# Gated linear attention: each head's scores from its own 32 partitions, four token tiles at once, in place of block-diagonal queries

## The chip, the cores and the metric

The kernel runs on one core of one Trainium2 chip. The metric is the device time of one execution in microseconds (us). Three runs of the kernel before took 2882.11, 2879.14 and 2889.37 us; their median is 2882.11 us.

## The reference, cut to what matters

The program is a chain of transformer layers over 512 tokens of 1024 features: two hybrid layers ("block 1"), then two further layers with a second stream of 256 context tokens. The change touches one part of each of the two hybrid layers, the gated linear attention of four heads with 32 key features and 64 value features each:

```python
def gated_linear_attention(q, k, v, log_a):      # S = 512, H = 4, Dk = 32, Dv = 64
    qc, kc, vc, gc = to_chunks(q * (Dk ** -0.5)), to_chunks(k), to_chunks(v), to_chunks(log_a)
    def step(state, inp):
        b = jnp.cumsum(gi, axis=2)
        rel = b[:, :, :, None, :] - b[:, :, None, :, :]
        decay = jnp.where(causal, jnp.exp(jnp.minimum(rel, 0.0)), 0.0)
        sc = jnp.einsum('bhid,bhijd,bhjd->bhij', qi, decay, ki)
        intra = jnp.einsum('bhij,bhjv->bhiv', sc, vi)
        inter = jnp.einsum('bhid,bhdv->bhiv', qi * jnp.exp(b), state)
        ...
```

So the score of query i and key j of a head is a sum over 32 features of q times k times a decay that differs by feature and by the pair (i, j), for j not after i; the output is these scores times the values.

## The kernel before, in words

All large products are done in float32r as three matmuls: an operand x is split into a high part (ScalarE casts it, `split`, lines 389 to 394) and a low part (x minus the high part, on GpSimd by line 385 or on VectorE by line 387), and high*high, high*low and low*high are added up in PSUM (`mms`, line 378). Line 376 is the one matmul call of all of them, so groups are told apart by their tiles.

In `layer1` (line 1187) the projections, the retention heads and the gated linear attention of a hybrid layer are laid out together: `weave` (called at line 1258) takes the steps of two generators in turn, `gla` against a chain of `project1`, `project2` and `retention`. The numbers there say how many steps each is reckoned to have, and how far ahead some may be scheduled. With every step `tick` (line 347) also lays out some of the background work, the modulations: `mods` (line 689) brings rows of a weight matrix through three buffers `mr` (one DMA of 256 KB each, line 702) and multiplies them on VectorE (`dot`, line 679). Every engine, and the queue SP that issues all these DMAs, works off its own list in order.

`gla` (line 999) holds queries and keys as [128 = (head, 32 features), 512 tokens]. Decays between two tokens of one tile of 128 tokens are made from seven levels of halving, and an eighth part (level 7 in the code) is the diagonal itself. For a level, keys and queries are multiplied by their decay factors (GpSimd, `prod`, line 1074), and all scores of the level are computed and the right ones kept by a mask: `copy_predicated` (line 1093) takes them from PSUM into A, a tile `oy` of [128 keys, 4 heads x 128 queries] for each token tile.

The heads share the 128 partitions, so the queries are spread out: `level` (line 1050) writes each head's 32 partitions of the queries into its own 128 columns of a tile `qb` that is zero elsewhere (four casts on ScalarE at line 1058, four subtractions on VectorE at line 1059, each 32 partitions x 256). `pair` (line 1062) then multiplies 128x128 keys by 128x512 block-diagonal queries, three matmuls for the four heads of one token tile, into one PSUM bank of the tag "b". `diagonal` does two token tiles at a time (HT = 2), 16 of these half levels in all, each one's matmuls laid out after the next one's preparation (`lagged`, line 302). The four tiles `qb` are filled with zeros first (line 1025). Six further pairs of token tiles (query tile after key tile) are computed the same way, without a mask (lines 1098 to 1115). At last the scores are split in two parts and multiplied by the values (lines 1117 to 1121) into two wide PSUM tiles (tag "s", two banks each, two of them), whose two halves of rows are added by `halves` (lines 883 and 886).

The PSUM tags are shared: "b" (two banks) also takes the scores of `retention` (line 1144) and the decay sums (line 1035); "s" also takes `dense_tok` (line 427), which in `project1` holds both wide tiles at once; "d" takes the projections and the sums of `retention`. In all, `gla` lays out 22 steps per layer.

Of the kernel before, what the change touches and what calls it, by code (L numbers as in the profile page):

```python
# [24 lines left out]
S = 512  # L25
# [9 lines left out]
# column offsets of the projections  # L35
# [70 lines left out]
# 1 / 10000 ** linspace(0, 1, 32) as float32 arithmetic gives it  # L106
# [13 lines left out]
def _consts():  # L120
# [17 lines left out]
    # rows are queries, columns keys  # L138
# [49 lines left out]
class Net:  # L188
# [40 lines left out]
    def area(self, pool, name, **bufs):  # L229
        """Allocator of a stream's attention tiles, by kind."""  # L230
# [5 lines left out]
    def flat(self, shape):  # L236
        """A bank of a wide tile."""
# [64 lines left out]
    def lagged(self, blocks, front=0, back=0):  # L302
        """blocks: generators of two steps; each one's second step comes after the next one's first."""
# [30 lines left out]
    def ahead(self, n):  # L334
        """What is laid out inside may be scheduled n instructions ahead of its place."""
# [11 lines left out]
    def tick(self):  # L347
        """Advances the work in the background."""
# [9 lines left out]
    def stage(self, low=3, **ahead):  # L358
        """low: one of so many low parts of weights is the vector engine's; how far ahead some kinds of work may go."""
# [22 lines left out]
    def lo(self, out, src, hi, scale=1.0, eng="pool"):  # L382
        """out = src * scale - hi"""
# [12 lines left out]
    def split_ps(self, src, hi, lo, scale=1.0):  # L396
        """The source lies in PSUM."""
# [16 lines left out]
    def dense(self, src, h, T, ks=range(KD), tag="d"):  # L414
        """One tile of 128 output features: [128, T] in PSUM."""
# [11 lines left out]
    def dense_tok(self, src, h, T, n, per):  # L427
        """n output features with tokens on partitions: a [128, n] PSUM view per token tile."""
# [16 lines left out]
    def three(self, ps, w, hs):  # L445
        """w: (hi, lo) stationary operands per k tile; hs: (hi, lo) moving ones."""
# [7 lines left out]
    def rstd_cols(self, sq_tiles, T, groups, width, add=False, al=None):  # L454
        """rstd per token (and per group of features) with tokens on partitions: [128, T/128, n]."""
# [17 lines left out]
    def spread(self, cols, T, reps=None, al=None):  # L473
        """[128, T] PSUM tile: per-token values of [128, T/128, n] in every row of their group."""
# [1450 lines left out]
```

## Time and profile before

| | before |
|---|---|
| median of three runs | 2882.11 us (2879.14 to 2889.37) |
| profiled execution, span | 2893.2 us |
| instructions | 33615 |
| TensorE busy (matmul) | 2371.8 us, 82% |
| VectorE busy | 1634.0 us, 56% |
| ScalarE busy | 1171.0 us, 40% |
| GpSimd busy | 1125.4 us, 39% |
| mean granted TensorE clock | 0.896 |

The profile tells one execution, whose only time is its span, 11.1 us (0.4%) above the median of the runs. Its shares are averages over stages with different limits. A matmul's recorded duration includes the pipeline behind it, so the pace of matmuls is read from the distance between their starts, not from their durations. A wait names what ended it last; what ended it may have been held up by something else.

### The profile page before, as it was taken

How to read it: one execution, taken by the hardware profiler on the slowest of the kernel's cores; microseconds unless marked ns; L12 is line 12 of the kernel's file. 1: busy time of each engine (PE TensorE's matmuls, PEld its weight loads, DVE VectorE, ACT ScalarE, POOL GpSimd, SP SyncE). 2: the span in 40 equal slices, each digit the busy share in tenths (PEclk: the TensorE clock that was granted, in tenths of full speed). 3: DMA queues.
4: the chain of work that ended last, by engine and by line, in shares of the span. 5: the costliest groups of instructions: out<-in, count | busy, mean ns of one | idle time of the engine just before them, and what ended most of it. 6: DMA issues, size and time to landing. Idle time of an engine off the chain costs nothing. (4 is left out here: it accounts for less than half of the span.)

```text
span 2893.2 us, 33615 instructions
## 1 busy us (share of the span) xinstructions
PE 2371.8 (82%) x11676; PEld 1960.4 (68%) x11676; DVE 1634.0 (56%) x2822; ACT 1171.0 (40%) x2167; POOL 1125.4 (39%) x754
## 2 busy tenths in 40 slices
PE   5866687668888876668999888999878969799997
PEld 4654565556667665457998776788766757588886
DVE  8777697267747897356452697622635647421212
ACT  3433264334537533345554522222434536332222
POOL 3445245325533652122444742333541221433334
PEclk9978698889979876779999998999988979899999
DMA  6553554354344544324654556632443254332322
GB/s 237 189 182 117 177 169 151 117 161 145 114 118 142 187 160 156 107 92 118 184 156 146 175 172 211 208 95 88 158 136 98 87 159 113 113 113 98 96 95 73
DMA packets 190111, 405.70 MB, mean 140 GB/s; under 512 B 21011, under 2 KB 62453, under 8 KB 186613
## 3 DMA queue, kind: packets, MB, share of 16 engines
q1 hardware_dynamic: 189940, 403.55, 43.4%
q8 instruction: 93, 1.52, 0.2%
q14 instruction: 78, 0.63, 0.1%
HBM read 345.08 MB, written 58.39 MB: 139 GB/s over the span
## 5 line engine op out<-in xcount | busy, mean ns | idle before, releaser
L385 POOL TENSOR_TENSOR wl<-wr,wh 128x1024 fp32r<-128x1024 f32 (+3 forms) x245 | 547.2, 2235 | 839.3 <-ACT wh L409 486.0
L409 ACT CAST wh<-wr 128x1024 fp32r<-128x1024 f32 (+3 forms) x367 | 353.7, 964 | 621.5 <-PE d L376 273.5
L376 PE MATMUL d<-hh,wh 128*128 128x512 f32 x960 | 402.6, 420 | 50.5 <-ACT wh L409 28.9
L376 PE MATMUL d<-hl,wh 128*128 128x512 f32 x960 | 401.0, 418 | 10.5 <-POOL hl L385 7.7
L679 DVE SCALAR_TENSOR_TENSOR mr<-mr,row 128x512 f32<-128x512 f32 x256 | 229.7, 905 | 76.9 <-DMA mr<-in_ada_w 39.0
L376 PEld LDWEIGHTS d<-hh,wh 128*128 128x128 f32 x960 | 194.5, 203 | 98.1 <-ACT wh L409 31.1
L376 PE MATMUL d<-hh,wl 128*128 128x512 f32 x960 | 256.7, 397 | 4.7 <-DVE wl L387 3.4
L387 DVE SCALAR_TENSOR_TENSOR wl<-wr,wh 128x1024 fp32r<-128x1024 f32 (+3 forms) x122 | 154.2, 1264 | 165.5 <-PE d L376 93.1
L376 PEld LDWEIGHTS d<-hl,wh 128*128 128x128 f32 x960 | 193.8, 202 | 56.5 <-POOL hl L385 12.6
L376 PEld LDWEIGHTS d<-hh,wl 128*128 128x128 f32 x960 | 181.9, 191 | 44.3 <-DVE wl L387 5.3
L387 DVE SCALAR_TENSOR_TENSOR pg<-b,pg 128x512 fp32r<-128x512 f32 (+1 forms) x208 | 136.9, 664 | 64.5 <-ACT pg L391 63.0
L892 POOL TENSOR_TENSOR oy<-pg,pg 64x256 f32<-64x256 f32 (+1 forms) x72 | 65.6, 911 | 273.9 <-DVE pg L890 123.5
L376 PE MATMUL b<-hh,wh 128*128 128x512 f32 x416 | 165.4, 398 | 0.0
L376 PE MATMUL b<-hl,wh 128*128 128x512 f32 x416 | 164.4, 395 | 0.0
L391 ACT CAST pg<-b 128x512 fp32r<-128x512 f32 (+1 forms) x208 | 117.3, 570 | 87.5 <-PE b L867 80.4
L840 DVE TENSOR_REDUCE sm<-s 128x1 f32<-128x768 f32 (+3 forms) x144 | 120.5, 845 | 57.0 <-PE s L376 56.5
L679 DVE SCALAR_TENSOR_TENSOR mj<-mr,row 128x512 bf16<-128x512 f32 x128 | 113.0, 882 | 34.5 <-DMA mr<-in_ada_w 34.5
L376 PE MATMUL d<-hc,wh 128*128 128x256 f32 x656 | 106.1, 314 | 26.3 <-ACT wh L409 12.3
L376 PE MATMUL d<-hid,wh 128*128 128x512 f32 (+1 forms) x528 | 116.9, 366 | 10.0 <-ACT hid L391 6.0
L376 PE MATMUL b<-qb,pg 128*128 128x512 f32 x228 | 80.5, 462 | 46.7 <-DVE oy L1093 13.7
L376 PEld LDWEIGHTS d<-hc,wh 128*128 128x128 f32 x656 | 96.0, 216 | 30.8 <-ACT wh L409 13.7
L376 PE MATMUL b<-hh,wl 128*128 128x512 f32 x416 | 108.6, 403 | 9.9 <-DVE wl L387 9.9
(414 smaller groups left out, 5210.5 us busy)
## 6 DMA issues: line engine op xcount, KB each, us to landing
wr<-in_ffn_w_in SPq DMA_DIRECT2D x132, 512.0 KB
mr<-in_ada_w SPq DMA_DIRECT2D x192, 256.0 KB
wr<-in_ffn_w_out SPq DMA_DIRECT2D x48, 512.0 KB
x<-x SPq DMA_DIRECT2D x20, 1024.0 KB
wr<-in_w_in SPq DMA_DIRECT2D x38, 512.0 KB
mr<-in_w_mod SPq DMA_DIRECT2D x64, 256.0 KB
wr<-in_ev_w_in SPq DMA_DIRECT2D x20, 512.0 KB
wr<-in_ffn_w_out SPq DMA_DIRECT2D x24, 384.0 KB
```

The source lines that it names most:

```text
L376: self.nc.tensor.matmul(out, lhsT, rhs, start=start, stop=stop)
L385: self.nc.gpsimd.tensor_sub(out, src, hi)
L387: self.nc.vector.scalar_tensor_tensor(out, src, scale, hi, op0=ALU.mult, op1=ALU.subtract)
L391: self.nc.scalar.copy(hi, src)
L409: nc.scalar.copy(hi[:, :n], raw[:, :n])
L679: self.nc.vector.scalar_tensor_tensor(junk, w, 0.5, v, op0=ALU.mult, op1=ALU.mult, accum_out=out)
L840: nc.vector.reduce_max(c, s, axis=AX.X, negate=True)
L892: nc.gpsimd.tensor_tensor(d, sel(t), sel(rs), op=ALU.mult)
```

## The change

`gla` is written anew from its zero tile on. No block-diagonal queries are made: the level's keys and queries of all four token tiles are split whole (128 x 512, four instructions), and a matmul reads 32 partitions of keys and 32 of queries, one head at a time, into 128 columns. Two heads (`y`: heads 0 and 1, or 2 and 3) and four token tiles fill a wide PSUM tile of the tag "s", and one `copy_predicated` of 128 x 1024 takes it. The six pairs of different token tiles are made two heads at a time in banks of the tag "b", and their parts are gathered by key tile (384, 256 and 128 queries). The scores tile `acc` is now laid out by head. The number of steps stays 22: 16 and 2 times 3. The rest of the diff takes out comments and an unused variable. Its core:

```diff
-        HT = 2
-        qblk = [[self.tl(ph, [128, HT, 4, 128], F32R, f"qb{i}{j}", 1) for i in range(2)] for j in range(2)]
-        for qb in qblk:
-            for q_ in qb:
-                for t in range(HT):
-                    nc.vector.tensor_copy(q_[:, t], A[0])
+        new_r = lambda: self.tl(ph, [128, S], F32R, "gh", 8)
+        new_z = lambda: self.tl(ph, [128, NT, 128], F32, "z", 2)
...
         def level(zk, zq):
-            kh, kl = self.pg([128, N2], F32R), self.pg([128, N2], F32R)
+            kh, kl, qh, ql = (new_r() for _ in range(4))
             self.split(zk, kh, kl)
-            qb = qblk[count[0] % 2]
-            count[0] += 1
-            for h in range(4):
-                r = slice(32 * h, 32 * h + 32)
-                nc.scalar.copy(qb[0][r, :, h, :], v4(zq[r]))
-                self.lo(qb[1][r, :, h, :], v4(zq[r]), qb[0][r, :, h, :], eng="dve" if h in [0, 1, 2, 3] else "pool")
-            return kh, kl, qb
-
-        def pair(lv, jk, jq):
-            kh, kl, qb = lv
-            ps = self.bank([128, 4, 128])
-            c = slice(jk * 128, jk * 128 + 128)
-            fl = lambda a: a.rearrange("p h t -> p (h t)")
-            self.mms(fl(ps), [(kh[:, c], fl(qb[0][:, jq])), (kh[:, c], fl(qb[1][:, jq])), (kl[:, c], fl(qb[0][:, jq]))])
-            return ps
+            self.split(zq, qh, ql, 1.0, "dve")
+            return (kh, qh), (kh, ql), (kl, qh)
+
+        def scores(lv, outs, jk, jq, n, first, last):
+            for i, (a, b) in enumerate(lv):
+                for h, o in outs:
+                    r = slice(32 * h, 32 * h + 32)
+                    self.mm(o, a[r, tok(jk)], b[r, tok(jq, n)], first and i == 0, last and i == 2)
...
-            for t in range(HT):
-                nc.vector.copy_predicated(A[t0 + t], m, pair(lv, t, t))
-
-        yield from self.lagged(diagonal(lvl, t0) for lvl in (7, 0, 1, 2, 3, 4, 5, 6) for t0 in range(0, NT, HT))
+        def diagonal(lvl, lv, y):
+            w = self.wide()
+            for t in range(NT):
+                scores(lv, [(2 * y + x, w[:, x, tok(t)]) for x in range(2)], t, t, 1, t == 0, t == NT - 1)
+            m = self.gla_mask[:, lvl, None, :].to_broadcast([128, 2 * NT, 128])
+            v8 = lambda a: a.rearrange("p h (t i) -> p (h t) i", i=128)
+            nc.vector.copy_predicated(v8(acc[:, 2 * y:2 * y + 2, :]), m, v8(w))
+
+        fs, last = {}, None
+        for lvl in (7, 0, 1, 2, 3, 4, 5, 6, None):
+            lv = None if lvl is None else prepare(lvl)
+            if last is not None:
+                for y in range(2):
+                    diagonal(*last, y)
+                    yield
+            last = lvl, lv
...
+        parts = [((0, 0, 1), (2, 2, 2)), ((3, 2, 2),), ((1, 1, 1),)]
+        for y in range(2):
+            sums = self.wide()
+            hs = (2 * y, 2 * y + 1)
+            v = lambda t, h: gv[t][:, h].rearrange("p a d -> p (a d)")
+            for h in hs:
+                hl = new_r(), new_r()
+                self.split(acc[:, h, :], *hl)
+                for t in range(NT):
                     for i in range(2):
-                        self.mm(acc[h // 2][:, h % 2, q0:q0 + n], v, hl[i][:, h, :],
-                                jt == 0 and i0 == 0 and i == 0, jt == NT - 1 and i == 1)
-                yield
-        for h in range(4):
-            self.halves(acc[h // 2][:, h % 2, :], [(o[h // 2][64 * (h % 2):64 * (h % 2) + 64], lambda a: a)], S)
+                        self.mm(sums[:, h % 2, tok(t)], v(t, h), hl[i][:, tok(t)], t + i == 0, False)
+            yield
+            for jt in range(3):
+                n = (3 - jt) * 128
+                ps = [self.bank([128, n]) for _ in hs]
+                c = 0
+                for jk, jq, m in parts[jt]:
+                    scores(lv, [(h, ps[x][:, c:c + m * 128]) for x, h in enumerate(hs)], jk, jq, m, c == 0, c + m * 128 == n)
+                    c += m * 128
+                for x, h in enumerate(hs):
+                    hl = self.pg([128, n], F32R), self.pg([128, n], F32R)
+                    self.split_ps(ps[x], *hl)
+                    for i in range(2):
+                        self.mm(sums[:, h % 2, (jt + 1) * 128:], v(jt, h), hl[i], False, jt == 2 and i == 1)
+                if jt == 0:
+                    yield
+            for h in hs:
+                self.halves(sums[:, h % 2, :], [(o_[h // 2][64 * (h % 2):64 * (h % 2) + 64], lambda a: a)], S)
+            yield
```

## Rows read from the trace of the kernel before

**Rows 1.** The page's groups: the matmuls with block-diagonal queries, both layers (count, busy us, mean ns).

```profile
L376 PE MATMUL b<-qb,pg 128*128 128x512 f32 x228 | 80.5, 462 | 46.7 <-DVE oy L1093 13.7 <-DVE qb L387 11.8 <-ACT f L1039 11.8
```

**Rows 2.** Busy us by engine in both stages; then clock, DMA share, GB/s.

```profile
105.00:319.00 214.00, 152.30 (x599) 118.67 (x597) 159.76 (x288) 80.56 (x163) 100.72 (x89) 0.82 0.51 160
583.00:816.00 233.00, 176.66 (x786) 141.31 (x785) 154.33 (x263) 96.75 (x192) 108.37 (x95) 0.90 0.44 139
```

**Rows 3.** VectorE's groups, first layer's stage: busy us, mean ns | idle before, releasers.

```profile
L679 DVE SCALAR_TENSOR_TENSOR mr<-mr,row 128x512 f32<-128x512 f32 x57 | 48.3, 864 | 36.1 <-DMA mr<-in_w_mod 35.9
L387 DVE SCALAR_TENSOR_TENSOR qb<-pg,qb 32x256 fp32r<-32x256 f32 x64 | 41.2, 643 | 8.1 <-ACT qb L1058 6.5
L1093 DVE COPY_PREDICATED oy<-gla_mask,b 128x512 f32<-128x512 uint8 x32 | 22.5, 725 | 2.0 <-PE b L376 1.7
L387 DVE SCALAR_TENSOR_TENSOR rp<-rp,rp 128x512 f32<-128x512 f32 x9 | 9.3, 1031 | 0.3
...
L387 DVE SCALAR_TENSOR_TENSOR A<-b,A 128x512 fp32r<-128x512 f32 x6 | 4.0, 686 | 5.1 <-ACT A L391 5.1
...
L387 DVE SCALAR_TENSOR_TENSOR rp<-s,rp 128x256 fp32r<-128x256 f32 x4 | 1.7, 420 | 0.5 <-ACT rp L391 0.4
```

**Rows 4.** The same view of VectorE, second layer's stage.

```profile
L387 DVE SCALAR_TENSOR_TENSOR qb<-pg,qb 32x256 fp32r<-32x256 f32 x64 | 42.1, 658 | 7.5 <-ACT qb L1058 6.0
```

**Rows 5.** Line 1025 by itself, both layers: count, ns min/median/max.

```profile
L1025 DVE CAST qb<-oy x16: 416/418/420, 81.3 to 584.6; 128x512 fp32r<-128x512 f32 x16
```

**Rows 6.** ScalarE's groups, first layer's stage.

```profile
L1058 ACT CAST qb<-pg 32x256 fp32r<-32x256 f32 x64 | 25.8, 402 | 6.5 <-POOL pg L1074 5.4
...
L391 ACT CAST pg<-pg 128x256 fp32r<-128x256 f32 x19 | 7.7, 406 | 29.7 <-POOL pg L1074 17.1 <-DVE pg L1148 7.3 <-DVE qb L387 5.0
...
L391 ACT CAST A<-oy 128x512 fp32r<-128x512 f32 x4 | 2.5, 618 | 8.9 <-PE s L376 5.4 <-DVE oy L1093 3.5
```

**Rows 7.** Timeline of PE, four stretches: start us, us (first start to last end).

```profile
102.86 0.63 PE L376 MATMUL d<-hl,wh 128*128 128x512 f32 x1
103.42 0.71 PE L376 MATMUL b<-gw,pg 16*128 16x128 f32 x2
...
105.09 0.38 PE L376 MATMUL b<-gw,pg 16*128 16x128 f32 x2
105.31 0.38 PE L376 MATMUL b<-gb,ones_row 1*128 1x128 f32 x2
105.62 0.50 PE L376 MATMUL d<-hh,wh 128*128 128x512 f32 x1
...
161.09 1.56 PE L376 MATMUL b<-qb,pg 128*128 128x512 f32 x6
...
811.70 0.33 PE L376 MATMUL s<-A,v 128*128 128x128 f32 x2
```

**Rows 8.** Timeline of the weight loads (PEld): four with one matmul of 128 columns each.

```profile
810.73 0.52 PEld L376 LDWEIGHTS s<-A,v 128*128 128x128 f32 x4 [0.84 <-POOL A L385]
```

**Rows 9.** PE's waits, first layer's stage: us in total, times, longest us.

```profile
PE b L376 <- DVE oy L1093: 14.3, 5, 8.5
PE b L376 <- DVE qb L387: 10.6, 3, 8.1
```

**Rows 10.** PE's waits, second layer's stage.

```profile
PE b L376 <- ACT f L1039: 11.8, 1, 11.8
PE b L376 <- DVE oy L1093: 8.4, 4, 6.0
```

**Rows 11.** Timeline of the first layer, 161 to 173 us: the longest wait of PE.

```profile
166.18 0.69 DVE L679 SCALAR_TENSOR_TENSOR mr<-mr,row 128x512 f32<-128x512 f32 x1 [4.22 <-DMA mr<-in_w_mod]
...
171.90 1.65 PE L376 MATMUL b<-qb,pg 128*128 128x512 f32 x3 [8.55 <-DVE oy L1093]
```

**Rows 12.** Timeline of the second layer: the last `halves` of gla, and of retention.

```profile
818.10 0.68 DVE L886 TENSOR_TENSOR oy<-s,pg 64x512 f32<-64x512 f32 x1 [0.38 <-ACT pg L883]
...
829.24 0.68 DVE L886 TENSOR_TENSOR oy<-d,pg 64x512 f32<-64x512 f32 x1
```

More of the change, by code (lines that the diff above doesn't have):

```diff
@@ L1015, in gla @@
         acc = self.tl(self.sb, [128, 4, S], F32, "oy", 2)
-        A = [acc[:, t, :].rearrange("p (h i) -> p h i", h=4) for t in range(NT)]
-        for t in range(NT):
-            nc.gpsimd.memset(A[t], 0.0)
-        HT = 2
-        qblk = [[self.tl(ph, [128, HT, 4, 128], F32R, f"qb{i}{j}", 1) for i in range(2)] for j in range(2)]
-        for qb in qblk:
-            for q_ in qb:
-                for t in range(HT):
-                    nc.vector.tensor_copy(q_[:, t], A[0])
+        for h in range(4):
+            nc.gpsimd.memset(acc[:, h, :], 0.0)
         tot = self.sm([128, 2])
         fx = self.tl(ph, [128, 2, 128], F32, "fx", 1)
+        new_r = lambda: self.tl(ph, [128, S], F32R, "gh", 8)
+        new_z = lambda: self.tl(ph, [128, NT, 128], F32, "z", 2)
         def factors(p):
             f = self.tl(ph, [128, NT, 3, 128], F32, "f", 1)
-            late = []
             w = self.gla_w[:, p * 3:p * 3 + 3, :].rearrange("p l t -> p (l t)")
@@ L1077, in gla @@
-        qv, kv = v4(q), v4(k)
-        fs = {}
-        def diagonal(lvl, t0):
-            if 0 <= lvl < 7 and lvl % 3 == 0 and t0 == 0:
-                fs[0] = factors(lvl // 3)
-            m = self.gla_mask[:, lvl, None, :].to_broadcast([128, 4, 128])
-            ts = slice(t0, t0 + HT)
-            if lvl == 7:
-                lv = level(k[:, t0 * 128:t0 * 128 + N2], q[:, t0 * 128:t0 * 128 + N2])
-            else:
-                fl = fs[0][:, ts, lvl % 3, :]
-                every = slice(0, HT)
-                lv = level(prod([(every, kv[:, ts], fl)]), prod([(every, qv[:, ts], fl)]))
-            yield
-            for t in range(HT):
-                nc.vector.copy_predicated(A[t0 + t], m, pair(lv, t, t))
@@ L1095, in gla, with prepare @@
-        yield from self.lagged(diagonal(lvl, t0) for lvl in (7, 0, 1, 2, 3, 4, 5, 6) for t0 in range(0, NT, HT))
+            self.split(zq, qh, ql, 1.0, "dve")
[5 more added lines that the diff above has]
+                    self.mm(o, a[r, tok(jk)], b[r, tok(jq, n)], first and i == 0, last and i == 2)
+        def prepare(lvl):
+            if lvl == 7:
+                return level(k, q)
+            if lvl % 3 == 0:
+                fs[0] = factors(lvl // 3)
+            zk, zq = new_z(), new_z()
+            for z, x in ((zk, kv), (zq, qv)):
+                nc.gpsimd.tensor_tensor(z, x, fs[0][:, :, lvl % 3, :], op=ALU.mult)
+            flat = lambda a: a.rearrange("p t i -> p (t i)")
+            return level(flat(zk), flat(zq))
@@ L1103, in gla @@
-        acc = [self.wide() for _ in range(2)]
-        for jt in range(NT):
-            for i0 in range(jt - jt % 2, NT, 2):
-                its = range(max(i0, jt), i0 + 2)
-                n = len(its) * 128
-                hl = [self.tl(ph, [128, 4, n], F32R, "A", 2) for _ in range(2)]
-                for x, it in enumerate(its):
-                    w = slice(x * 128, x * 128 + 128)
-                    if it == jt:
-                        self.split(A[jt], hl[0][:, :, w], hl[1][:, :, w])
-                    else:
-                        i, ck, cq = where[jt, it]
-                        self.split_ps(pair(lv[i], ck, cq), hl[0][:, :, w], hl[1][:, :, w])
-                q0 = its[0] * 128
-                for h in range(4):
-                    v = gv[jt][:, h].rearrange("p a d -> p (a d)")
-                    for i in range(2):
-                        self.mm(acc[h // 2][:, h % 2, q0:q0 + n], v, hl[i][:, h, :],
-                                jt == 0 and i0 == 0 and i == 0, jt == NT - 1 and i == 1)
-                yield
@@ L1123, in gla @@
-        for h in range(4):
-            self.halves(acc[h // 2][:, h % 2, :], [(o[h // 2][64 * (h % 2):64 * (h % 2) + 64], lambda a: a)], S)
+        zk, zq = new_z(), new_z()
+        for o, a, b in ((zk[:, 0:2], kv[:, 0::2], suf[:, 0::2]), (zq[:, 0:2], qv[:, 1::2], pre[:, 1::2]),
+                        (zk[:, 2], kv[:, 0], fx[:, 0]), (zk[:, 3], kv[:, 1], suf[:, 1]),
+                        (zq[:, 2], qv[:, 2], pre[:, 2]), (zq[:, 3], qv[:, 3], fx[:, 1])):
+            nc.gpsimd.tensor_tensor(o, a, b, op=ALU.mult)
```

18 lines of the change are left out of this document (4 added, 14 removed).

## Prediction, made before the changed kernel was seen

> **What bounds the kernel now.** I read the page's groups first: the score matmuls of gated linear attention are 228 of 11676, so what the change can move lies in two stages, one per hybrid layer [rows 1]. The busy time by stretch then shows what each stage is short of [rows 2]. In the first layer VectorE works 159.8 of 214 us; the groups of VectorE add 35.9 us in which it stood at the head of its queue waiting for a modulation row [rows 3]. That is 195.7 us, 91% of the stage: its queue sets the pace, and PE (152.3 us, 71%) has 62 us idle. In the second layer PE is the busier one, 176.7 of 233 us (76%), with 56 us idle; VectorE has 154.3 us (66%). The waits of PE show what of its idle time belongs to gated linear attention: in the first layer 14.3 us ended by the masked copy and 10.6 us by the query low parts [rows 9], in the second 11.8 us by the decay exponentials and 8.4 us by the masked copy [rows 10]. The longest of them is not that copy's own doing: PE stood 8.55 us until 171.90, and VectorE, which had to make that copy, had itself waited 4.22 us for a row before 166.18 [rows 11].
>
> The sums are made on a trace of 2893.2 us span, its only time, 11.1 us above the median 2882.1; I put the differences on the median. About 0.3% (8.6 us) is what a measurement of this kernel can tell from no change.
>
> **VectorE, per layer.** Removed: 9 levels x 2 halves x 4 heads = 72 low parts at 0.643 us [rows 3], 46.3 us; 32 masked copies at 0.725 us, 23.2; 8 zero fills at 0.418 us [rows 5], 3.3; 6 low parts of the off-diagonal scores at 0.686 us, 4.1. Sum 76.9 us. Added: 9 low parts of 128x512. The same operation on this shape took 1.031 us in this stage and 0.686 us at its quickest row [rows 3]; I take the first, 9.3 us. 16 masked copies of 1024 columns, a shape the trace does not have: from 256 to 512 columns a low part grew from 0.420 to 0.686 us, 0.266 us per 256, so 0.725 + 0.532 = 1.26 us, 20.1 us; ends 0.725 us (a second bank for nothing) and 1.45 us (twice the row). The off-diagonal low parts keep their 3072 columns but come in 12 pieces, 6 more fixed parts of 0.420 - 0.266 = 0.154 us: 5.0 us. Sum 34.4, saved 42.5 us. The second layer has 0.658 us per query low part [rows 4]: 43.6 us. If the old query parts had cost no more than 0.42 us of real work (the 256-column row), it would be 26 us.
>
> **ScalarE, per layer.** 72 query casts at 0.402 us and 18 key casts at 0.406 us go (36.2 us), 18 casts of 128x512 at 0.618 us come (11.1 us), with 6 more fixed parts of 0.194 us (0.406 less 0.212 for 256 columns): 24 us saved [rows 6]. It is busy 38 to 42% [rows 2], so by itself that is worth nothing; it shortens the chain in front of the scores. GpSimd's products and key low parts keep their columns in half as many pieces; I count nothing. No DMA is added or moved, and the steps stay 22, so the interleaving with projections, retention and modulations is laid out as before.
>
> **PE.** The old 228 matmuls ran at (1.56 - 0.40) / 5 = 0.23 us at full clock [rows 7]: 52 us in both layers. The new ones: 8 levels x 2 x 4 tiles x 3 x 2 heads = 384 per layer, and 48 off the diagonal, 864 in both, 816 of them 128 columns wide. The columns are the same 58368 per layer; what is new is a weight load for every 128 columns and 32 partitions instead of 128. How fast two heads on different partitions follow each other the trace does not show. Upper end: four loads in 0.52 us, one being 0.19, are 0.11 us apart [rows 8], and matmuls of 16 and of 1 partitions also came 0.11 us apart (0.22 for two) [rows 7]. Lower end: half of it, two heads in the time of one, 0.055 us. The pair of 128-column matmuls at 811.70 whose loads were in started 0.06 us apart (0.33 us in all, 0.27 the second) [rows 7]; I take 0.06 us, since two heads' loads are into different rows, which gives 864 x 0.06 = 52 us and no difference. The value products keep 10240 columns per layer in 56 pieces, not 48: +1 us.
>
> Changing between matmuls of 128 partitions and of few costs extra: into the few, 0.56 us from 102.86 to 103.42 against 0.43 us for 512 columns at that half clock, +0.13; out of them, the last start at 105.42 to 105.62 is 0.20 against 0.11, +0.09 [rows 7]. So 0.22 us for in and out. The old scores are 38 groups per layer; I take as many changes, 8.4 us per layer (ends 22 groups unbroken, 5 us; every pair alternating with a projection, 216 changes, 48 us). The Trainium skill's TensorEngine Tiling (Array Packing), Key Properties, says that changing the tiling mode drains the engine. The rows agree in sign; the page has no price, and by an undrained change the sum would be 12 us lower.
>
> **Banks.** The masked scores move from the tag "b" to the wide tiles. `dense_tok` holds both for some 40 us per layer, in which up to 12 score matmuls (2.7 us) must go elsewhere; retention and the decay sums get "b" to themselves. Both are within the ends; I count nothing.
>
> **What of it is on the path.** First layer: VectorE is 91% of the path, but its queue also holds the rows' multiplications, which must wait for their DMA through three buffers; with less work between them they wait longer. Ends: all 42 us, or none. I take half, -21 us. Second layer: PE's idle time that this work ends is 20 us of 56 [rows 10]; half, -10 us, about a quarter of VectorE's saving. Retention's last sum is at 829.24, 11 us after that of gated linear attention at 818.10 [rows 12]: it is late next. PE's additions, 9.4 us per layer, count by its busy share, 0.71 and 0.76: +14 us. Sum -17: **2865 us**.
>
> **The rivals.** *Heads do not overlap (slower).* Each 128-column matmul then costs its load, 0.11 us: 864 x 0.11 = 95 us, 43 more than now, 21.6 per layer; by the busy shares 15 + 16 = +32, so 2897 us. Against it stands PE's 62 us idle in the first layer; for it, every row of short matmuls that has a load each. It decides from 17 / (864 x 0.735) = 0.027 us above my price: 0.087 us per matmul. The Trainium skill's TensorE: Matmul & The Clock Gate says under LDWEIGHTS that a load takes time by columns, whatever its rows, which is this case; under Part 3 that matmuls of different row groups start about 4 ns apart, which by the 0.11 us row is 0.057 us each and the forecast. No row here separates them.
>
> *The modulation rows take it back.* VectorE is done sooner but then waits for the row; 35.9 us of such waits grow by 18, the first layer gains 3: 2883 us. For it: the waits are already the largest group. Against it: 57 rows in 214 us are one per 3.75 us, 11 us for three buffers, and the wait of 4.22 us is far shorter.
>
> *The queue was all of it.* All 42 us of the first layer and half of the second's count: -42 - 21 + 14 = -49, 2833 us.
>
> **Chances.** Forecast 0.45 (four fifths of it faster by over 0.3%), overlap missing 0.22, rows take it back 0.16, queue was all of it 0.17. Faster 0.36 + 0.17 = 0.53; within 0.3%: 0.09 + 0.13 + 0.03 = 0.25; slower 0.19 + 0.03 = 0.22. The range takes in both outer rivals: 2830 to 2903 us; the forecast's own, with changes of mode at 5 to 17 us per layer, is 2848 to 2879.
>
> **What would show it.** Right: VectorE busy near 117 us in the first stage and 111 in the second; masked copies near 1.26 us; two heads' matmuls starting nearly together, 24 in about 1.5 us at full clock. Wrong: 24 in 2.6 us or more; PE busy over 175 us in the first stage; the rows' wait near 54 us; or retention ending later than before, whatever gated linear attention does.

## The result, and the profile after

The changed kernel takes 3023.8 us (median of four runs, 3020.9 to 3028.7) against 2881.9 for the kernel before on the same chip: a ratio of 1.0485, 95% interval 1.0465 to 1.0505. It is 142 us slower; the prediction was 2865, with a range up to 2903. The two profiled executions in the table differ by 129 us only, since that of the kernel before lies 11 us above its median; lengths of stages below are taken from the traces.

| | before | after |
|---|---|---|
| profiled execution, span | 2893.2 us | 3022.0 us |
| instructions | 33615 | 34456 |
| TensorE busy | 2371.8 us, 82% | 2504.9 us, 83% |
| VectorE busy | 1634.0 us, 56% | 1559.2 us, 52% |
| ScalarE busy | 1171.0 us, 40% | 1120.7 us, 37% |
| mean granted TensorE clock | 0.896 | 0.863 |

VectorE did lose the work it was meant to lose. Its groups over the whole program (count, busy us, mean ns | idle before, releasers), as against [rows 3]:

```profile
L1074 DVE COPY_PREDICATED oy<-gla_mask,s 128x1024 f32<-128x1024 uint8 x32 | 41.5, 1302 | 39.3 <-PE s L376 39.3
```

The masked copy of 1024 columns took 1.30 us, predicted 1.26. But VectorE now stands 39.3 us waiting for PE ahead of these copies. The score matmuls, from the same view, answer to [rows 1]:

```profile
L376 PE MATMUL s<-gh,gh 32*128 32x128 f32 x768 | 110.2, 355 | 25.8 <-DVE oy L1074 22.6 <-DVE rp L387 3.2
```

768 of the 864 are in this group. The stages of gated linear attention are now 100 to 443 us and 670 to 959 us. The busy time by stretch of the changed kernel (us, then each engine's busy us, granted clock, DMA share, GB/s), with 25 us of the first stage by themselves:

```profile
100.00:443.00 343.00, 265.94 (x981) 185.06 (x982) 168.58 (x325) 67.84 (x121) 101.93 (x70) 0.63 0.42 133
106.00:131.00 25.00, 25.00 (x63) 15.78 (x62) 10.96 (x22) 9.13 (x12) 3.85 (x2) 0.58 0.34 106
...
670.00:959.00 289.00, 230.30 (x1215) 187.58 (x1213) 121.28 (x198) 80.52 (x143) 107.96 (x77) 0.77 0.36 115
```

The same view of the kernel before, for its own two stages and the same 25 us:

```profile
106.00:131.00 25.00, 23.88 (x104) 18.72 (x102) 22.94 (x36) 16.54 (x29) 17.37 (x15) 1.00 0.55 175
...
100.00:346.00 246.00, 166.37 (x652) 130.18 (x653) 181.03 (x331) 90.80 (x182) 110.39 (x94) 0.79 0.54 169
574.00:830.00 256.00, 195.79 (x892) 157.74 (x891) 162.47 (x280) 106.73 (x213) 115.69 (x100) 0.90 0.41 131
```

The first stage is 97 us longer and the second 33; everything after them is as long as before (2063 us to the end in both). In each stage PE's busy time grew by as much as the stage, and the granted clock fell, from 0.79 to 0.63 and from 0.90 to 0.77. In the 25 us PE was busy throughout and got 63 matmuls done in place of 104. The timeline of PE in the changed kernel shows what it was doing there and a little later (start us, us from first start to last end):

```profile
106.61 0.80 PE L376 MATMUL d<-hh,wh 128*128 128x512 f32 x1
107.33 0.47 PE L376 MATMUL s<-gh,gh 32*128 32x128 f32 x1
107.73 0.80 PE L376 MATMUL d<-hl,wh 128*128 128x512 f32 x1
108.46 0.47 PE L376 MATMUL s<-gh,gh 32*128 32x128 f32 x1
...
132.42 0.32 PE L376 MATMUL s<-gh,gh 32*128 32x128 f32 x1
132.68 0.50 PE L376 MATMUL d<-hh,wh 128*128 128x512 f32 x1
133.11 0.32 PE L376 MATMUL s<-gh,gh 32*128 32x128 f32 x1
```

Each score matmul of 32 partitions is followed by one projection matmul of 128 partitions, and so on: from 106.61 to 107.73 such a pair takes 1.12 us, at 132.42 to 133.11 it takes 0.69. In PE's list of instructions the 864 score matmuls lie in 187 unbroken stretches, 121 of them a single matmul; the 228 of before lay in 76. Counted by the starts in the trace, as in the table below, the changed kernel has 190, since a few of its matmuls start ahead of their place in the list.

The table below splits each stage by PE's records. The time from one matmul's start to the next one's, less PE's idle time, is put down to the first of the two: either a score matmul or one of the others (projections, retention, decay sums, values). The others are nearly the same work in all kernels, 534 to 550 matmuls in the first stage and 774 to 782 in the second. A stage is taken to end with the transposes of line 485 that follow it. Each cell is first stage / second stage, in us; the kernels below the second row are the experiments.

| kernel | stretches | score matmuls | other matmuls | PE idle | length |
|---|---|---|---|---|---|
| before | 49 / 27 | 37 / 32 | 129 / 164 | 80 / 60 | 246 / 256 |
| after | 142 / 48 | 77 / 43 | 189 / 187 | 77 / 59 | 343 / 289 |
| full128 | 142 / 45 | 57 / 62 | 140 / 171 | 96 / 57 | 293 / 290 |
| before_short | 133 / 42 | 71 / 67 | 143 / 170 | 77 / 54 | 292 / 291 |
| before_rows32 | 46 / 27 | 45 / 40 | 149 / 181 | 66 / 49 | 260 / 270 |
| prio500 | 27 / 13 | 51 / 45 | 148 / 181 | 74 / 59 | 273 / 285 |
| quad500 | 20 / 24 | 40 / 32 | 152 / 182 | 75 / 60 | 268 / 274 |
| two500 | 20 / 14 | 37 / 32 | 150 / 177 | 64 / 63 | 253 / 272 |
| before_two | 37 / 26 | 25 / 23 | 140 / 168 | 79 / 63 | 246 / 255 |

Of the 130 us that the two stages grew, 51 lie in the score matmuls and 83 in the matmuls that the change doesn't touch; idle time is 4 us less.

### The profile page after: what moved, and what is told of

The parts are those of the page before. It is cut to its first block, busy times and chain, and to the rows that moved or that the text cites. A ratio compares the mean times of both kernels' runs of the same rounds, so it can differ in the third digit from the quotient of the medians.

```text
span 3022.0 us, 34456 instructions
## 1 busy us (share of the span) xinstructions
PE 2504.9 (83%) x12328; PEld 2041.6 (68%) x12328; DVE 1559.2 (52%) x2660; ACT 1120.7 (37%) x2035; POOL 1107.2 (37%) x708
## 5 line engine op out<-in xcount | busy, mean ns | idle before, releaser
L376 PE MATMUL d<-hh,wh 128*128 128x512 f32 x960 | 417.5, 436 | 43.8 <-ACT wh L409 20.6
L376 PE MATMUL d<-hl,wh 128*128 128x512 f32 x960 | 415.9, 434 | 10.0 <-POOL hl L385 8.2
L376 PE MATMUL d<-hh,wl 128*128 128x512 f32 x960 | 277.4, 416 | 5.1 <-DVE wl L387 3.9
L387 DVE SCALAR_TENSOR_TENSOR pg<-b,pg 128x512 fp32r<-128x512 f32 (+3 forms) x232 | 146.3, 639 | 88.3 <-ACT pg L391 86.9
L391 ACT CAST pg<-b 128x512 fp32r<-128x512 f32 (+3 forms) x232 | 125.1, 549 | 119.1 <-PE b L867 78.4
L376 PEld LDWEIGHTS s<-gh,gh 32*128 32x128 f32 x768 | 82.7, 248 | 80.9 <-issue 67.2
L376 PE MATMUL s<-gh,gh 32*128 32x128 f32 x768 | 110.2, 355 | 25.8 <-DVE oy L1074 22.6
L908 DVE SCALAR_TENSOR_TENSOR rp<-rp,d 128x512 f32<-128x512 f32 (+1 forms) x77 | 46.8, 608 | 140.7 <-ACT rp L907 140.6
```

The source lines that it names most:

```text
L376: self.nc.tensor.matmul(out, lhsT, rhs, start=start, stop=stop)
L387: self.nc.vector.scalar_tensor_tensor(out, src, scale, hi, op0=ALU.mult, op1=ALU.subtract)
L391: self.nc.scalar.copy(hi, src)
L908: nc.vector.scalar_tensor_tensor(t, t, 1.0, ps, op0=ALU.add, op1=ALU.mult)
```

## The experiments

Theory 1: the loss is the change between matmuls of 128 and of 32 partitions, made dear by the order in which the two kinds alternate. Rivals: many short matmuls hold the clock at its lower level, whatever their partitions (theory 2), or cost a weight load each (theory 4); the wide PSUM tiles, which the projection with tokens on partitions also wants, hold things up (theory 3). Theory 5 concerns the saving that did not come: VectorE's time is hidden, and PE's counts nearly in full. The kernel before took 2882 to 2886 us beside these runs.

### The same matmuls in another order: prio500, prio30, critical

In prio500 the score matmuls of a block are laid out 500 instructions ahead of their place, in prio30 by 30; in critical the block is closed to other work.

```diff
-            for t in range(NT):
-                scores(lv, [(2 * y + x, w[:, x, tok(t)]) for x in range(2)], t, t, 1, t == 0, t == NT - 1)
+            with self.ahead(500):      # prio30: self.ahead(30); critical: self.tc.tile_critical()
+                for t in range(NT):
+                    scores(lv, [(2 * y + x, w[:, x, tok(t)]) for x in range(2)], t, t, 1, t == 0, t == NT - 1)
```

The six pairs off the diagonal are put in the same bracket.

> The changed kernel with the score matmuls laid out 500 instructions ahead of their place, which leaves 40 stretches of 32-partition matmuls on PE instead of 187, without fences. Theory 1: 2900 to 2975 us. Theory 2: within 20 us of 3024. Theory 3: within 20 us of 3024, since the tiles and their order of use are the same.

> The same with 30 instructions ahead: 266 stretches instead of 187, of which 196 are a single matmul. Theory 1: 79 more changes at 0.34 to 0.70 us, 27 to 55 us more than the changed kernel: 3050 to 3080. Theories 2 and 3: within 20 us of 3024.

> The changed kernel with the score matmuls of a group (24 of a wide tile, or those of a key tile) fenced so that nothing else comes between them on PE: 39 stretches of 32-partition matmuls instead of 187. Theory 1: some 150 changes fewer at 0.34 us (full clock) to 0.70 us (half clock) each, 50 to 105 us less: 2920 to 2975, less any cost of the fences themselves. Theory 2: within 20 us of 3024. Theory 3: within 20 us of 3024.

Measured: prio500 2948.7 us, 1.0224 [1.0196, 1.0253], with 40 stretches; prio30 3075.4 us, 1.0663 [1.0633, 1.0693], with 266 (272 by the starts in the trace); critical 3001.2 us, 1.0401 [1.0372, 1.0430], with 39. So the order alone, with not one matmul more or less, moves the time over 127 us. Stage by stage it goes by the stretches: in the first, 27, 81 and 142 stretches (prio500, prio30, after) take 273, 295 and 343 us; in the second, 13, 48 and 191 (prio500, after, prio30) take 285, 289 and 385. From the least to the most that is 0.61 and 0.56 us per stretch, though not evenly: from 13 to 48 the second stage grows by 4 us only. Critical has the stretches of prio500, is 52 us above it and over theory 1's range; its bracket puts 44 branches and 44 drains more into PE's list, and PE's idle time in the two stages is 96 and 90 us (74 and 59 in prio500), so it tells nothing more of theory 1. In prio500 an unbroken stretch looks like this (timeline of PE):

```profile
195.69 1.56 PE L376 MATMUL s<-gh,gh 32*128 32x128 f32 x24
```

24 matmuls, a load each, in 1.56 us: (1.56 - 0.32) / 23 = 0.054 us each, half the 0.11 us of a load [rows 8]. So two heads do overlap. The Trainium skill's TensorE: Matmul & The Clock Gate, Part 3, says that matmuls of different row groups run at once; this stretch agrees. It holds only as long as no projection lies between the two.

### Partitions or number: full128, before_short, before_rows32

full128 is the changed kernel with each score matmul over all 128 partitions, in the same order; its scores then sum over the heads.

```diff
-                    r = slice(32 * h, 32 * h + 32)
+                    r = slice(0, 128)
```

> The changed kernel with each score matmul over all 128 partitions instead of its head's 32 (so the scores are sums over all four heads); every engine's list of instructions is in the same order as in the changed kernel. Theory 1 (the time goes into changing between matmuls of 32 and of 128 partitions, which alternate one by one on PE): no changes are left, 864 matmuls cost their weight load of 0.11 us at full clock, 43 us more than before instead of about 140: 2880 to 2915 us. Theory 2 (many short matmuls hold the clock at its lower level, whatever their rows): stays within 40 us of 3024. Theory 3 (the masked scores in the wide PSUM tiles hold back the projection that uses them, and the reverse): stays above 2960.

before_short is the kernel before with four matmuls of 128 columns for each one of 512, all over 128 partitions:

```diff
-            self.mms(fl(ps), [(kh[:, c], fl(qb[0][:, jq])), (kh[:, c], fl(qb[1][:, jq])), (kl[:, c], fl(qb[0][:, jq]))])
+            prods = ((kh, qb[0]), (kh, qb[1]), (kl, qb[0]))
+            for i, (kk, qq) in enumerate(prods):
+                for h in range(4):
+                    self.mm(ps[:, h, :], kk[:, c], qq[:, jq, h, :], i + h == 0, i + h == 5)
```

> The kernel before with its block-diagonal queries, its order, its banks and its masked copies as they were; only each 512-column score matmul becomes four of 128 columns over all 128 partitions, 228 becoming 912, each with its own weight load. Theory 4 (the number of matmuls and loads is the loss that is left once the mode changes are gone): a 128-column matmul with a load costs its load, 0.11 us, so the scores take 912 x 0.11 = 100 us in place of 52, 48 more, at half clock up to twice that; by a busy share of 0.75 +36 us, 2915 to 2950. Theory 3 (what is left comes from the banks): the banks are those of before, so within 10 us of 2884.

before_rows32 is the kernel before with the same 228 matmuls of 512 columns over 32 partitions:

```diff
+            r = slice(0, 32)
-            self.mms(fl(ps), [(kh[:, c], fl(qb[0][:, jq])), (kh[:, c], fl(qb[1][:, jq])), (kl[:, c], fl(qb[0][:, jq]))])
+            self.mms(fl(ps), [(kh[r, c], fl(qb[0][r, jq])), (kh[r, c], fl(qb[1][r, jq])), (kl[r, c], fl(qb[0][r, jq]))])
```

> The kernel before, in which each of its 228 score matmuls keeps its 512 columns and its place but goes over the first 32 partitions only (the scores of heads 1 to 3 are left out). It has no more matmuls, loads or columns, and the same 76 stretches; only the number of partitions changes, so it prices the change between kinds of matmul alone. Theory 1 (an in-and-out costs 0.34 us at full clock, 0.70 at half): 76 x 0.34 to 0.70 = 26 to 53 us of PE, and with nine tenths of it counting, as in the runs so far, 2907 to 2932. The prediction's price (0.22 us, three quarters counting): +13, about 2898. Rival (the stretches of the changed kernel are dear for another reason, its short matmuls): 2884, within 6 us.

Measured: full128 2972.6 us, 1.0306 [1.0273, 1.0338]; before_short 2974.1 us, 1.0326 [1.0296, 1.0356]; before_rows32 2920.2 us, 1.0118 [1.0099, 1.0138]. full128 lies 58 us above theory 1's range and 11 us below theory 2's; of the three only theory 3's "above 2960" fits, which bank500 takes up below. Each effect exists by itself. The number of matmuls costs 88 us in the structure of before, more than theory 4 expected (its order changed with it, from 76 stretches to 175); the partitions cost 34 us there, in the range of theory 1 and well over the prediction's 13. In the changed kernel's order the partitions cost 51 us, after against full128. And full128 with all parts of the change but the 32 partitions stands where before_short stands with none but the short matmuls: the VectorE work saved and the other parts are together worth nothing that shows there.

The timeline of PE in full128 shows the same alternation as after, with 128 partitions on both sides:

```profile
112.09 0.22 PE L376 MATMUL s<-gh,gh 128*128 128x128 f32 x1
112.15 0.44 PE L376 MATMUL d<-hl,wh 128*128 128x512 f32 x1
112.43 0.22 PE L376 MATMUL s<-gh,gh 128*128 128x128 f32 x1
```

A pair takes 0.34 us. In either kernel 94 score matmuls stand singly between two projections of 512 columns. From the one projection's start to the next one's it is 0.34 or 0.35 us (70 of them) or 0.64 (16) in full128, and 0.68 or 0.69 us (21) or 1.12 or 1.13 (66) in after. By the granted clock at their starts the shorter value of each belongs to the full clock (2.4 GHz), the longer to the half (1.2 GHz). At the full clock full128's pair is the sum of 0.11 and 0.23 us, so alternating by itself costs nothing there. One in-and-out costs 0.34 us at full clock and 0.49 at half, and after stands at half clock for most of them where full128 stands at full. The clock of full128 in the same 25 us, from its busy time by stretch:

```profile
106.00:131.00 25.00, 24.65 (x117) 20.43 (x116) 18.13 (x29) 11.61 (x16) 12.02 (x8) 0.89 0.50 162
```

0.89, and 117 matmuls, against 0.58 and 63. That a lower clock goes with few partitions is seen again in before_rows32, where the number, the columns and nearly all places of the matmuls are those of before (busy time by stretch):

```profile
100.00:360.00 260.00, 194.32 (x651) 134.48 (x649) 176.19 (x329) 90.29 (x180) 106.80 (x94) 0.74 0.50 159
587.00:857.00 270.00, 220.67 (x897) 167.66 (x896) 160.42 (x281) 107.63 (x213) 114.82 (x100) 0.82 0.39 124
```

0.74 and 0.82 in place of 0.79 and 0.90. Its timeline of PE gives the price for long matmuls:

```profile
125.14 0.50 PE L376 MATMUL b<-qb,pg 32*128 32x512 f32 x1
125.57 0.50 PE L376 MATMUL d<-hh,wl 128*128 128x512 f32 x1
126.00 0.50 PE L376 MATMUL b<-qb,pg 32*128 32x512 f32 x1
```

A pair of 512 columns each takes 0.86 us, where two at 0.23 would take 0.46: 0.40 us for in and out. The Trainium skill's TensorEngine Tiling (Array Packing), Key Properties, has the array drain at such a change; these rows agree in that a change costs time, and give the price.

In before_short the timeline of PE shows what a short matmul costs between longer ones:

```profile
142.39 0.22 PE L376 MATMUL b<-qb,pg 128*128 128x128 f32 x1
142.45 0.39 PE L376 MATMUL s<-wh,hh 128*128 128x384 f32 x1
142.68 0.22 PE L376 MATMUL b<-qb,pg 128*128 128x128 f32 x1
```

A pair takes 0.29 us. Among themselves the short ones start 0.11 us apart at full clock and 0.21 at half (some 730 such distances, median 0.113): a load each, four times per 512 columns that took 0.23. By the table the scores take 138 us there in place of 69, and the others 20 us more.

### Banks and overlap: bank500, full128_500

bank500 is prio500 with the diagonal scores in two single banks in place of a wide tile:

```diff
-            w = self.wide()
+            w = [self.bank([128, S]) for _ in range(2)]
...
-            m = self.gla_mask[:, lvl, None, :].to_broadcast([128, 2 * NT, 128])
-            v8 = lambda a: a.rearrange("p h (t i) -> p (h t) i", i=128)
-            nc.vector.copy_predicated(v8(acc[:, 2 * y:2 * y + 2, :]), m, v8(w))
+            m = self.gla_mask[:, lvl, None, :].to_broadcast([128, NT, 128])
+            for x in range(2):
+                nc.vector.copy_predicated(v4(acc[:, 2 * y + x, :]), m, v4(w[x]))
```

> The changed kernel, 500 ahead, with the diagonal scores of a pair of heads in two of the single banks in place of a wide tile, and each masked copy in two of 512 columns. Theory 3 (the wide tiles, which the projection with tokens on partitions wants as well, are the loss that is left): PE's waits for the masked copy at that projection (22.6 and 20.3 us) go, and it is 20 to 45 us under the 2949 of the same order with wide tiles: 2905 to 2930. Theory 4 (number of matmuls): within 10 us of 2949, or a little slower, since 32 more masked copies have their fixed part and the single banks are shared with retention.

full128_500 joins the edits of full128 and prio500.

> The changed kernel with its score matmuls over all 128 partitions and laid out 500 instructions ahead, 40 stretches and no change of mode at all (the scores are then sums over the heads). Theory 1 (mode changes, the dose being the stretches): with 40 stretches there is little left to gain over the 2949 of the same order with 32 partitions, 40 x 0.34 to 0.70 = 14 to 28 us, less what the loss of the heads' overlap gives back (two heads one after the other cost up to 864 x 0.05 = 43 us): 2920 to 2965. Theories 3 and 4 (banks; number of matmuls): it stays over 2920, since both are still there. If nothing but mode changes made the loss: under 2890.

Measured: bank500 2990.9 us, 1.0375 [1.0349, 1.0400]; full128_500 2986.8 us, 1.0351 [1.0304, 1.0398]. Theory 3 finds no support: without the wide tiles it is 42 us slower than prio500, not faster. PE's idle time in the two stages is 82 and 68 us in it, more than the 74 and 59 with the wide tiles. (The single banks are shared with retention, so this shows that they are no better, not that the wide tiles cost nothing.) full128_500 is 38 us slower than prio500 and over its expectation: where the stretches are long, the overlap of the heads is worth more than what the few changes of mode cost. Against full128 it is 14 us slower, but the two intervals overlap, so what the place 500 ahead costs by itself is not shown. The clock of full128_500, from its busy time by stretch:

```profile
100.00:374.00 274.00, 223.33 (x975) 198.07 (x976) 157.96 (x301) 67.28 (x120) 101.63 (x70) 0.70 0.48 157
604.00:922.00 318.00, 258.79 (x1209) 229.90 (x1210) 122.46 (x198) 81.22 (x144) 108.69 (x77) 0.76 0.32 105
```

prio500, the same order with 32 partitions, is granted no more (its busy time by stretch):

```profile
100.00:373.00 273.00, 198.74 (x976) 162.31 (x977) 158.06 (x300) 67.92 (x123) 101.81 (x70) 0.69 0.49 159
603.00:888.00 285.00, 226.19 (x1208) 192.20 (x1209) 125.13 (x199) 80.77 (x143) 107.51 (x76) 0.76 0.37 116
```

So the clock also falls below that of before where every score matmul has 128 partitions and is short, as theory 2 has it; few partitions are not the only thing that a lower clock goes with.

### What VectorE and PE are worth: before_low, before_nolow, before_two, low_first

before_low makes the queries' low parts once and lets ScalarE spread them; low_first does that in the first layer only.

```diff
+            qh, ql = self.pg([128, N2], F32R), self.pg([128, N2])
+            self.split(zq, qh, ql, 1.0, "dve")
             for h in range(4):
...
-                self.lo(qb[1][r, :, h, :], v4(zq[r]), qb[0][r, :, h, :], eng="dve" if h in [0, 1, 2, 3] else "pool")
+                nc.scalar.copy(qb[1][r, :, h, :], v4(ql[r]))
```

> The kernel before with its block-diagonal queries and all its matmuls; only the queries' low parts are taken once for 128 partitions on VectorE and spread over the heads by ScalarE. VectorE: per half level one 128x256 low part of 0.42 us for four at 0.643, 18 x 2.15 = 39 us less per layer; ScalarE: one cast and four copies more at 0.40, 18 x 2.0 = 36 us more per layer, to 117 and 133 us of the two stages. The prediction's reading of the path (half of VectorE's saving counts in the first layer, a quarter in the second): -19 and -10, 2850 to 2862. Rival a (VectorE's queue does not set the pace, its time is filled by waits for rows): 2875 to 2890. Rival b (ScalarE's longer chain in front of the scores becomes the wait): 2890 to 2920.

> A version that could beat both: the kernel before, with the queries' low parts made once and spread by ScalarE in the first layer only. In the run that did so in both layers the first stage took 237 us in place of 246 and the second 266 in place of 256. If those two are effects of the edit, the first layer alone gives -9, 2875; if they are only a shift of the steps against the transfers, within 5 us of 2884.

before_nolow puts `if h == 0:` in front of the low part; before_two drops `(kl[:, c], fl(qb[0][:, jq]))` from the three products.

> The kernel before without the low parts of the queries of heads 1 to 3 (those products stay zero): 18 x 3 x 0.643 = 35 us of VectorE less per layer, with nothing added on any engine and all matmuls as they were. The prediction's reading (VectorE's queue is 91% of the first stage's path: half of the saving counts there, a quarter in the second layer): -17 and -9, 2858. Its rival that the queue was all of it: -35 and -17, 2832. Theory 5 (VectorE's time is hidden behind PE and the waits for rows, which is why the run with the low parts made once stood at 2887): 2874 to 2888.

> The kernel before without the third product of the scores (low keys by high queries is left out): 76 matmuls of 512 columns fewer, at 0.23 to 0.43 us 17 to 33 us of PE, and nothing else changed. Theory 5 (in these stages PE's time counts nearly in full, since its idle time did not shrink in any run that gave it more work): -15 to -30, 2854 to 2870. The prediction's reading (PE's time counts by its busy share, 0.71 to 0.76): -12 to -25, so these two overlap. Rival (PE is not the bound; more work costs, less work gives nothing): 2878 to 2888.

Measured: before_low 2887.1 us, 1.0010 [0.9998, 1.0023]; before_nolow 2876.5 us, 0.9966 [0.9955, 0.9978]; before_two 2890.3 us, 1.0013 [0.9998, 1.0028]; low_first 2881.6 us, 0.9977 [0.9964, 0.9991]. before_low puts on ScalarE about what it takes off VectorE (ScalarE is busy 116.8 and 126.5 us in the windows of [rows 2], for 80.6 and 96.8), and before_nolow has no such payment: with 35 us of VectorE less per layer and nothing added, 9 us are gained, a third of what the prediction's reading of the path gives (26) and near the edge of what theory 5 does. In before_nolow the busy time by stretch, for the windows of [rows 2], is:

```profile
105.00:319.00 214.00, 153.13 (x630) 121.73 (x628) 136.48 (x259) 85.89 (x173) 101.35 (x91) 0.86 0.55 172
583.00:816.00 233.00, 187.50 (x805) 151.07 (x806) 121.80 (x217) 99.02 (x197) 112.13 (x98) 0.87 0.41 129
```

and its group of VectorE's row multiplications in the first of them:

```profile
L679 DVE SCALAR_TENSOR_TENSOR mr<-mr,row 128x512 f32<-128x512 f32 x62 | 57.2, 936 | 50.6 <-DMA mr<-in_w_mod 50.4
```

VectorE has 23 and 33 us less to do there, and its wait for the rows went from 35.9 to 50.4 us: 14.5 of the 23 us that it had gained in the first stage. In the second the wait for rows grew by 5 us only, from 13.9 to 18.7; why the rest counts for so little there is not shown.

before_two is the odd one. Its score matmuls take 21 us less of PE, but the others take 16 us more, and the stages are as long as before. The clock of the two stages, from its busy time by stretch:

```profile
100.00:346.00 246.00, 165.59 (x624) 129.20 (x625) 175.15 (x331) 92.24 (x183) 107.52 (x94) 0.77 0.55 172
575.00:830.00 255.00, 191.65 (x856) 154.30 (x856) 164.60 (x280) 105.53 (x212) 116.38 (x100) 0.86 0.41 131
```

0.77 and 0.86 for 0.79 and 0.90. So what theory 5 says of PE fails here: work added to PE was paid for, from over half in before_rows32 (of 52 us 28 by the traces, 34 by the medians) to nearly in full in after, and work taken away gave nothing here. low_first is faster than before by 0.23%, less than the 0.3% that a measurement of this kernel can tell from no change; so no version that does the whole work clearly beats it.

### What is left at prio500: quad500, two500

quad500 lets four heads follow each other over both wide tiles:

```diff
...
-            w = self.wide()
-            with self.ahead(500):
-                for t in range(NT):
-                    scores(lv, [(2 * y + x, w[:, x, tok(t)]) for x in range(2)], t, t, 1, t == 0, t == NT - 1)
+            if y == 0:
+                quad[:] = [self.wide(), self.wide()]
+                with self.ahead(500):
+                    for t in range(NT):
+                        scores(lv, [(h, quad[h // 2][:, h % 2, tok(t)]) for h in range(4)], t, t, 1, t == 0, t == NT - 1)
+            w = quad[y]
...
```

The lines with a minus are those of prio500, whose bracket around the six pairs off the diagonal stays. two500 is prio500 without `(kl, qh)` among the products that `level` returns.

> The changed kernel, 500 ahead, with all four heads in turn over both wide tiles, 48 stretches' worth of diagonal scores joined into stretches of 96, so that four heads on four groups of 32 partitions can overlap where two did. If the 65 us that were left at 2949 are the time of the 864 matmuls themselves (some 83 us of PE in the two stages, from one start to the next): half of it goes, 2900 to 2925. If four overlap no better than two, or if the rest lies in the order and the clock: 2940 to 2960. If both wide tiles at once make PE wait for the masked copies, or the projection that needs the same tiles: over 2960.

> The changed kernel, 500 ahead, without the third product of the scores (low keys by high queries is left out), so 576 score matmuls in place of 864. If the 65 us that were left are the matmuls' own time: 288 x 0.1 = 29 us of PE less, 2915 to 2930. If taking matmuls away gives nothing back, as in the kernel before (2890 against 2886, the clock of the other matmuls fell instead): 2940 to 2955.

Measured: quad500 2934.4 us, 1.0184 [1.0160, 1.0207]; two500 2917.5 us, 1.0128 [1.0107, 1.0148]. (quad500's stretches are of 48 matmuls in place of 24, not of 96 as its expectation has it.) In two500, where 29 us of matmuls were expected to come off, 31 did, so there the number counted in full. Four heads overlap better than two, as the timelines of PE of quad500 and prio500 show, both at half clock:

```profile
209.13 3.71 PE L376 MATMUL s<-gh,gh 32*128 32x128 f32 x48
```

```profile
211.86 2.82 PE L376 MATMUL s<-gh,gh 32*128 32x128 f32 x24 [6.83 <-DVE oy L1075]
```

Less the last one's duration, 0.47 us at that clock as at 107.33 above, that is (3.71 - 0.47) / 47 = 0.07 us each against (2.82 - 0.47) / 23 = 0.10: better, not half, and 14 us less in the time, between the two outcomes that were expected. What it does settle is in the table: in quad500 the score matmuls take 72 us in both stages, 3 more than in before, and yet the two stages are 40 us longer (52 by the medians). Those 40 us are in the other matmuls (152 and 182 for 129 and 164 us), at a lower clock (busy time by stretch of quad500):

```profile
100.00:368.00 268.00, 192.03 (x980) 156.17 (x981) 157.51 (x292) 68.45 (x124) 102.65 (x70) 0.69 0.50 165
598.00:872.00 274.00, 213.87 (x1209) 173.85 (x1210) 121.38 (x198) 81.14 (x144) 108.25 (x77) 0.79 0.38 121
```

Why the clock is granted less, beyond its going with matmuls of few partitions in before_rows32 and with short ones in full128_500, these runs don't show.

## Why the prediction was wrong

**The step that failed: the number of changes between kinds of matmul.** "The old scores are 38 groups per layer; I take as many changes, 8.4 us per layer." The new scores are 142 and 48 stretches. The old order mixed long matmuls with long matmuls of the same kind, so it did not matter there where the two streams met; I carried the number of meetings over, without asking how two streams of equal place are merged when one has four times as many matmuls; before_short, four times the matmuls in the old structure, goes from 76 stretches to 175 as well. The bad end was on paper (every pair alternating, 216 changes, 48 us per layer), and the first layer, with 142, went most of the way to it; put into the sum it gives 2923 us, and the range ended at 2903. The order alone is worth 75 of the 159 us that were missed (after against prio500). The rest is not in the number: prio500, with 40 stretches where 76 were counted, is still 84 us over the forecast, its PE records having grown by some 63 us where 19 were counted, and VectorE's saving of 31 us not having come.

**The price per change** was 0.22 us; it is 0.34 (short matmuls) to 0.40 (long ones) at full clock and 0.49 at half. My figure came from the one place where the decay's matmuls of 16 and 1 partitions meet a projection [rows 7], put together a way in at half clock and a way out at full clock, and was used for all. What the clock does to the other matmuls was in no term. Of the 83 us that these grew by, PE's records give as an estimate some 38 to the ones directly in front of a score matmul (189 for 76), over what the same shape takes elsewhere at the same clock, and some 47 to the clock: 475 of 1329 start at half clock, where 194 of 1315 did before. Per stretch, with the clock, a stage lost 0.56 to 0.61 us from one order to another.

**The price per matmul** of 0.06 us holds only in an unbroken stretch with two heads in turn (0.054). A projection in between ends the overlap, and each way in and out comes on top. The rival "heads do not overlap" had this mechanism and 0.11 us, but priced it at +32 us; before_short, which comes nearest to that mechanism alone, is +88. The difference is again the clock (0.21 us at half) and the weight of 0.71 to 0.76 for PE's work: in before_short the stages took 81 of the 89 us that PE's records grew by, in the changed kernel all but 4 of 134. PE's idle time in these stages hardly filled with the new matmuls; only in before_rows32 did it give way, by 25 us of 140.

**VectorE's path.** The busy times came out near what was worked out: 0.946 us per low part for 1.031, 1.30 per copy for 1.26, and in the second stage 41 us less in all for 43.6. Their value did not: -31 us counted; for before_nolow the same reading gives -26, and -9 was measured; before_low, which pays on ScalarE, gained nothing. The rival that the modulation rows take it back was right for this term in the first layer, with its mechanism: in before_nolow the wait for the rows grew by 14.5 us of the 23 that were freed. That VectorE's busy time plus its waits for rows is 91% of a stage did not make it the bound; that wait grew when the work around it shrank.

**Banks** were counted as nothing, and bank500 gives no sign against it. **Retention late next** held: the last `halves` of gated linear attention and of retention in the second layer (timeline of VectorE after, against [rows 12]) are

```profile
949.14 0.68 DVE L886 TENSOR_TENSOR oy<-s,pg 64x512 f32<-64x512 f32 x1 [0.19 <-ACT pg L883]
...
960.24 0.68 DVE L886 TENSOR_TENSOR oy<-d,pg 64x512 f32<-64x512 f32 x1
```

So retention again ends last, 11 us behind gated linear attention, and both end 131 us later than before. The sign of being wrong that named a later end of retention came true, together with PE's 266 us in the first stage for the 175 that were named.

## What to carry to other kernels

Before matmuls of fewer partitions are put in, look at what stands beside them in TensorE's order: one way in and out cost 0.34 to 0.49 us here, and more of the neighbours ran at half clock, so they belong in long unbroken stretches, with the heads in turn. Even then they did not pay here: the best such order, quad500, is 1.8% slower than the long matmuls over all partitions. Splitting a matmul of 512 columns into four of 128 cost a load each (0.11 us at full clock) unless two heads on different partitions followed each other directly (0.054). And work saved on an engine that waits for DMAs is worth what a run with that work simply left out says, here a third of the estimate.

## What was not expected

Matmuls over 32 partitions went with a lower granted clock although TensorE is busy all the time: 0.58 against 0.89 in the same 25 us and the same order with 128 partitions, and 0.74 and 0.82 against 0.79 and 0.90 when little but the partitions of 228 matmuls changes. It is not the partitions alone: full128_500 has 0.70 and 0.76 with all 128. Leaving out 76 matmuls of the kernel before gained nothing: the clock of the two stages fell, from 0.79 to 0.77 and from 0.90 to 0.86, and the other matmuls took 16 us more.
